# Features-first product pairs: three of five additions replaced by accumulation onto ScalarE copies in PSUM

## The chip, the core and the metric

The kernel runs on one core of a Trainium2 chip. The metric is the device time of a run in microseconds, lower is better; it is given as the median of several runs.

## The reference, cut to what matters

One layer of a gated decoder trunk on 1024 prompt rows and 8 sample rows (1032 in all), width 1024. One input projection with seven blocks of 1024 columns gives u, v, z_a, x_b, z_b, g_a and g_b. Branch A mixes a normalised v within chunks of 128 rows; branch B pools x_b over trailing windows. Two more projections merge them, then an output projection, a norm, and a gate with a per-layer embedding follow.

```python
proj = einsum('bld,de->ble', rmsnorm(h, pre_g), w_in)
u, v, z_a, x_b, z_b, g_a, g_b = split(proj, ...)
vn = layernorm(gelu(v), ln_g, ln_b)
y_a = gelu(u) * chunk_spatial_mix(vn, w_s, b_s) * silu(z_a)
y_b = pooled(x_b) * silu(z_b)
m = sigmoid(g_a) * (y_a @ w_pa) + sigmoid(g_b) * (y_b @ w_pb)
h = h + rmsnorm(m @ w_out, post_g)
h = h + rmsnorm(sigmoid(rmsnorm(h, ple_in_g) @ w_pg) * (p @ w_ple), ple_out_g)
```

## The kernel before, in words

**The pairs.** Every large projection is cut into pairs of 128 output features (four pairs for each of the nine: v, ga, u, za, xb, zb, gb, pa, pb). The result of a pair is two features by two halves of the rows, 512 and 520 (WIDE, which holds the 8 sample rows). `strassen` (L691) computes it with Winograd's scheme: seven products P1 to P7 instead of eight, each a sum of weights (A11, A12, A22, S1 to S4) by a sum of the activations (B11, B21, B22, T1 to T4). P1, P2 and P4 have 512 columns, the other four 520, issued as two pieces of 260 (`Features.pieces`). `product` (L663) issues 4 contraction blocks by 3 terms, since each operand is split into a high and a low part (`split`: a ScalarE copy and a VectorE subtraction).

**What happens to a product.** `evacuate` inside `strassen` (L701): P1 is copied by ScalarE from PSUM to a slot u (with eight zero columns from `none`); P6 is added onto u by VectorE; P7 plus u gives u7; P5 plus u7, P4 plus u7 and P3 plus u are results (`user.summed`); P2 accumulates in PSUM onto P1 and goes out by ScalarE with the pair's function (`user.direct`). That makes five VectorE additions. `finish` then applies the function (gelu, silu, sigmoid or none for xb) to the results that came by `summed`. For pa and pb (`Merge`, L1322, `MergeB`, L1339) `direct` is a VectorE multiplication by a reloaded gate.

**PSUM.** Three regions of two banks (`region`, tag "acc") and two single banks (`bank`); they are taken in turn.

**The operand sums.** x, turned to features by rows, lies in `big` (128 by 8 by 1032). `combine` (L525) overwrites quarters of it in place: T3 = B22 - B12 over B22, T1 = B12 - B11 over B12, T2 = B11 + T3 over B11, T4 = B21 - T2 over B21; `cut` splits each into slots. After that `big` serves as scratch: the eight chunks of v (`vtok`, L1005) and their spatial mix (`spatial`, L1118), which `ZA` (L1193) multiplies in; the pooling windows (`XB.window`, L1256) with four scratch rows; and at the end the merged result.

**What sets the order.** Every operation is recorded by a planner (`Planner`, `order`, L274) which then lays out all five queues: it estimates durations, gives each operation a due time, and takes on each engine, TensorE too, what can start soonest and is due first. `PUSH` moves due times of named operations. `run_stream` (L833) records the steps one product after another; weights are prepared AHEAD = 3 steps before use, loads fetched 6 steps before. The first three pairs of v are interleaved by `MERGED` with the order `EDGE`; the start up to product 6 is written out in `SCRIPT`, with embedding products (`embed`, L1697) and the operand sums between. 46 slots of SBUF hold everything that is not in `big`. All SBUF loads and stores are issued on SP's queue, two kinds of accumulating ones on POOL's. Because all operations are recorded, nearly every row of the profile has line 374.

**Branch B.** The steps of group g are the pair xb, the pair zb and `mixes(g)` (L1285), two further products; `mixes` is placed after the third product of the next group's xb pair, and yb is spilled three steps later (`store`, L1423).

Of the kernel before, what the change touches and what calls it, by code (L numbers as in the profile page):

```python
# [31 lines left out]
PUSH = {'hs': -4.0, 'norm': -5.0, 'half': 0.0, 'cut': -1.0, 'e': 2.0, 'we': -2.0, 'vw': -9.0, 'p': 3.0}  # L32
# [8 lines left out]
OS, GS = 5, 12  # L41
WINDOWS = (2, 4, 8, 16)
# [339 lines left out]
def hybrid_step(  # L382
# [12 lines left out]
    accp = ctx.enter_context(tc.tile_pool(name="accp", bufs=3, space=bass.MemoryType.PSUM))  # L395
    bankp = ctx.enter_context(tc.tile_pool(name="bankp", bufs=2, space=bass.MemoryType.PSUM))
    plan = Planner(nc, SLOTS, {"acc": 3, "bank": 2})
# [64 lines left out]
    big = cpool.tile([P, NB, T], F32, tag="big", name="big")  # L462

# [35 lines left out]
    class Operand:  # L499
# [5 lines left out]
                    "T1": (0, 1), "T2": (0, 0), "T3": (1, 1), "T4": (1, 0)}  # L505
# [9 lines left out]
        def cut(self, what):  # L515
            i, j = self.QUARTERS[what]
            for kk in range(2):
                hi, lo = self.new(what, kk)
                if what == "T2":
                    split(quarter(kk, 0), hi[:, :, :HALF], lo[:, :, :HALF])  # L520
                    split(quarter(2 + kk, 1)[:, :, HALF:], hi[:, :, HALF:], lo[:, :, HALF:])
# [94 lines left out]
    class Features:  # L616

        new = staticmethod(lambda: region("acc"))
# [3 lines left out]
        @staticmethod  # L622
        def view(ps, wide):
            return ps[:, :, :QT] if wide else ps[:, 0, :HALF]

        @staticmethod
        def pieces(ps, wide):
            if not wide:
                return [(ps[:, 0, :HALF], slice(0, HALF))]
# [5 lines left out]
    class Tokens:  # L635

        new = staticmethod(lambda: region("acct")[:, 0])
# [53 lines left out]
    def strassen(weights, operand, user, form=Features, order=None):  # L691
# [41 lines left out]
        for p, a, b, r in sorted(plan, key=lambda x: order.index(x[0])) if order else plan:  # L733
            def run(p=p, a=a, b=b, r=r):
                new = r not in at
                if new:
                    at[r] = form.new()
                product(form, at[r], weights.ready[a], operand, b, new, True, not new)

            steps.append(Step(lambda a=a: weights.prepare(a), run, lambda p=p: evacuate(p)))  # L740
        steps[0].loads = lambda: (weights.fetch(), user.loads())
# [3 lines left out]
    def strassen_within(weights, operand, user, order=None):  # L745
# [26 lines left out]
        for p, a, b, r in sorted(plan, key=lambda x: order.index(x[0])) if order else plan:  # L772
            def run(a=a, b=b, r=r):
                new = r not in at
                if new:
                    at[r] = Tokens.new()
# [188 lines left out]
    def x_half(j, kps):  # L965

        for kp in kps:
            two = region("pst") if kp != 1 else None
            ps = [bank("pst") if two is None else two[:, kk] for kk in range(2)]
# [35 lines left out]
    vtok = lambda t: sv if t == S else big[:, t, :D]  # L1005
# [856 lines left out]
```

## Time and profile before

| | |
|---|---|
| median of 3 runs | 978.66 us (976.48 to 979.82) |
| profiled execution | span 975.6 us from its first to its last instruction; the page gives no other time of it |
| TensorE (PE) busy | 963.1 us, 99% |
| weight loads (PEld) | 855.9 us, 88% |
| VectorE (DVE) busy | 813.4 us, 83% |
| ScalarE (ACT) busy | 497.9 us, 51% |
| GpSimd (POOL) busy | 74.2 us, 8% |
| granted TensorE clock, mean | 0.998 (the upper level, 2.4 GHz) |
| DMA | 185.82 MB |

Times are microseconds unless marked ns. Matmuls overlap in the records: the pace is read from start to start, not from the length of one. An engine's busy share says little by itself; what counts is what it waits for and who waits for it. A name such as `xT2h,uw` reads: high part of operand sum T2, weights of a u pair; `acc` is a PSUM accumulator of a pair, `acct` one of the output and gate stages, `pst` the turning of x, `e` the embedding.

### The profile page before, as it was taken

The page shows a single profiled execution, that of the slowest core. Times are in us where ns is not written, and L with a number is a line of the kernel's source. Part 1 is how long each engine was busy: PE and PEld are TensorE (multiplying, and loading weights), DVE is VectorE, ACT ScalarE, POOL GpSimd, SP SyncE. Part 2 cuts the span into 40 slices and gives each one's busy share as a digit, 9 for nine tenths or more (in the row PEclk, how much of TensorE's full clock was granted, in tenths as well). Part 3 has the DMA queues.
Part 4 walks back from the last instruction along what each step waited for, and adds up shares of the span by engine and source line. Part 5 has one row for each costly group of instructions (what it writes and reads, how often), then busy time and mean ns, then how long its engine had stood idle before and what let it go on. Part 6 is the DMA issues. An engine that isn't in the chain of part 4 may idle for free. (4 is left out here: it accounts for less than half of the span.)

```text
span 975.6 us, 15918 instructions
## 1 busy us (share of the span) xinstructions
PE 963.1 (99%) x6037; PEld 855.9 (88%) x6037; DVE 813.4 (83%) x1261; ACT 497.9 (51%) x852; POOL 74.2 (8%) x117
## 2 busy tenths in 40 slices
PE   8999999999999999999999999999999999999996
PEld 6789899999999999999999999999999997788775
DVE  6998568988889788868698897698699899779987
ACT  7664345766444443242434343563263274698655
POOL 2200000000000000000010100000000001323212
PEclk9999999999999999999999999999999999999999
DMA  9523955423467464453425366692492385799896
GB/s 327 172 105 68 192 124 183 155 97 119 164 226 261 136 203 160 140 195 120 152 99 183 134 214 238 228 384 89 158 382 92 111 301 189 151 299 313 224 320 215
DMA packets 128506, 185.82 MB, mean 190 GB/s; under 512 B 42150, under 2 KB 85198, under 8 KB 128421
## 3 DMA queue, kind: packets, MB, share of 16 engines
q1 hardware_dynamic: 126381, 177.43, 54.9%
q0 software_dynamic: 2048, 7.37, 4.1%
q8 instruction: 47, 0.77, 0.3%
q14 instruction: 30, 0.25, 0.1%
HBM read 129.27 MB, written 55.96 MB: 190 GB/s over the span
## 5 line engine op out<-in xcount | busy, mean ns | idle before, releaser
L374 DVE TENSOR_TENSOR u<-acc,u 128x520 f32<-128x520 f32 (+1 forms) x89 | 62.0, 696 | 35.5 <-PE acc L374 35.2
L374 POOL TENSOR_TENSOR rstd<-ms,mhalf 128x1 f32<-128x1 f32 (+1 forms) x37 | 30.9, 841 | 520.3 <-DVE ms L374 517.7
L374 ACT ACTIVATE u<-acc 128x512 f32<-128x512 f32 (+1 forms) x43 | 25.6, 596 | 44.2 <-PE acc L374 44.0
L374 DVE TENSOR_TENSOR big<-big 128x1024 f32<-128x1024 f32 (+4 forms) x20 | 23.8, 1219 | 0.0
L374 POOL COPY big<-xb 128x1 f32<-128x1 f32 x8 | 3.4, 419 | 260.4 <-ACT xb L374 219.7
L374 ACT ACTIVATE paw<-pas 128x512 fp32r<-128x512 f32 x16 | 10.0, 630 | 24.0 <-DVE pas L374 18.2
L374 ACT ACTIVATE pbw<-pbs 128x512 fp32r<-128x512 f32 x16 | 10.0, 628 | 22.1 <-DVE pbs L374 16.8
L374 PE MATMUL accm<-qh,wpoolw 128*128 128x260 f32 (+1 forms) x96 | 20.9, 319 | 0.0
L374 ACT ACTIVATE big<-mix 128x256 f32<-128x256 f32 x32 | 12.0, 382 | 17.1 <-PE mix L374 16.4
L374 ACT ACTIVATE gbw<-gbs 128x512 fp32r<-128x512 f32 x16 | 10.1, 630 | 19.3 <-DVE gbs L374 10.0
L374 DVE SCALAR_TENSOR_TENSOR zb<-accm,gvec,zb 128x512 f32<-128x512 f32 (+1 forms) x16 | 12.0, 754 | 9.4 <-PE accm L374 9.2
L374 ACT ACTIVATE zaw<-zas 128x512 fp32r<-128x512 f32 x16 | 10.0, 628 | 18.1 <-DVE zas L374 10.0
L374 ACT ACTIVATE junk<-h 128x512 bf16<-128x512 f32 x25 | 15.7, 628 | 3.4 <-DVE h L374 2.9
L374 PEld LDWEIGHTS accm<-qh,wpoolw 128*128 128x128 f32 x96 | 15.6, 188 | 1.9
L374 ACT ACTIVATE zbw<-zbs 128x512 fp32r<-128x512 f32 x16 | 10.1, 628 | 13.8 <-DVE zbs L374 8.2
L374 ACT ACTIVATE u<-acct 128x512 f32<-128x512 f32 x22 | 13.0, 589 | 7.4 <-PE acct L374 4.6
L374 DVE TENSOR_TENSOR paw<-pas,paw 128x512 fp32r<-128x512 f32 x16 | 10.9, 688 | 6.7 <-ACT paw L374 6.7
L374 ACT ACTIVATE mw<-ms 128x512 fp32r<-128x512 f32 x16 | 10.0, 625 | 12.4 <-DVE ms L374 9.7
L374 ACT ACT_TABLE_LOAD x11 | 14.1, 1283 | 4.0 <-PE acc L374 2.3
L374 ACT ACTIVATE zbw<-zbraw 128x512 fp32r<-128x512 f32 x12 | 7.5, 623 | 16.6 <-DMA zbraw<-in_w_in_dram 10.7
L374 ACT ACTIVATE gbw<-gbraw 128x512 fp32r<-128x512 f32 x12 | 7.4, 624 | 16.4 <-DMA gbraw<-in_w_in_dram 14.3
L374 PE MATMUL mix<-wst,vh 128*128 128x256 f32 x64 | 15.5, 320 | 0.0
(655 smaller groups left out, 3560.5 us busy)
## 6 DMA issues: line engine op xcount, KB each, us to landing
ga<-ga SPq DMA_DIRECT2D x16, 516.0 KB, 4.6
gb<-gb SPq DMA_DIRECT2D x16, 516.0 KB, 6.2
ya<-za SPq DMA_DIRECT2D x8, 516.0 KB, 3.6
yb<-zb SPq DMA_DIRECT2D x8, 516.0 KB, 4.5
x<-in_x_prompt_dram SPq DMA_DIRECT2D x8, 512.0 KB, 9.3
vraw<-in_w_in_dram SPq DMA_DIRECT2D x8, 512.0 KB, 6.4
e<-e SPq DMA_DIRECT2D x8, 512.0 KB, 3.6
vturned<-v SPq DMA_DIRECT2D x32, 128.0 KB, 4.5
```

Of the source, the lines that this page charges most:

```text
L374: getattr(getattr(self.nc, e), method)(*(self.real(a) for a in args), **{k: self.real(a) for k, a in kwargs.items()})
```

## The change

A new function `seeded` takes the place of `strassen` for all pairs but the first three of v, in the order P1, P7, P6, P2, P5, P4, P3. ScalarE copies P1 from its single bank into a double one (in two pieces and eight zero columns), and P6, P5 and P3 accumulate there one upon the other; P7 is copied to a slot w. VectorE adds w to the double bank after P6 and writes the sum into the second single bank, upon which P4 accumulates. So P2, P4 and P3 go out by `direct`, P5 alone by `summed`. PSUM becomes two fixed double banks (`acc`), two fixed single ones (`one`) and two of `bank`. The operand sums are written differently (T1 first, then T2 = B22 - T1 over the same place, T3 = T2 - B11, T4 = B21 - T2), and B22 is not overwritten. The spatial mix is stored to DRAM chunk by chunk and loaded back by rows of features; the chunks and the window scratch use fewer rows of `big`. `mixes` stands after the whole next xb pair (LATE = 7), with its accumulators in `bank` and `acc`, and the store of yb right behind it. Evacuations of the new pairs are due 2.0 us earlier for the planner. The rest adapts names; the diff is cut to its core.

```diff
+PUSH = {..., 'out': 2.0}
+LATE = 7
+PST = (0, None, 2, 1)
...
-    plan = Planner(nc, SLOTS, {"acc": 3, "bank": 2})
+    plan = Planner(nc, SLOTS, {"bank": 2})
...
+    def banks(i):
+        return one if i == 2 else [acc[i][:, q] for q in range(2)]
...
-    def region(name):
-
-        n_name[0] += 1
-        return plan.tile(accp.tile([P, 2, 512], F32, tag="acc", name=f"{name}_{n_name[0]}"), "acc")
+    acc = [plan.tile(accp.tile([P, 2, 512], F32, tag=f"acc{i}", name=f"acc{i}"), "acc") for i in range(2)]
+    one = [plan.tile(accp.tile([P, 512], F32, tag=f"one{i}", name=f"one{i}"), "acc") for i in range(2)]
...
+    flat = big.rearrange("p b t -> p (b t)")
+    KEPT = 8 * WIDE
...
-                    "T1": (0, 1), "T2": (0, 0), "T3": (1, 1), "T4": (1, 0)}
+                    "T1": (0, 1), "T2": (0, 1), "T3": (0, 0), "T4": (1, 0)}
...
-                if what == "T3":
-                    sub(b22, b22, b12)
-                elif what == "T1":
+                if what == "T1":
                     sub(b12[:, :, :HALF], b12[:, :, :HALF], b11)
                 elif what == "T2":
-                    add(b11, b22[:, :, :HALF], b11)
+                    sub(b12, b22, b12)
+                elif what == "T4":
+                    sub(b21, b21, b12[:, :, :HALF])
                 else:
-                    sub(b21, b21, b11)
+                    sub(b11, b12[:, :, :HALF], b11)
...
     class Features:
-        new = staticmethod(lambda: region("acc"))
+        new = staticmethod(lambda wide: turn("wide", acc) if wide else turn("one", one))
...
     class Tokens:
-        new = staticmethod(lambda: region("acct")[:, 0])
+        new = staticmethod(lambda wide: turn("tokens", [one[0], acc[0][:, 0], one[1], acc[1][:, 0]]))
...
+    def seeded(weights, operand, user):
+
+        steps, at, cut = [], {}, (slice(0, QT), slice(QT, HALF))
+        plan_of = (("P1", "A11", "B11"), ("P7", "S3", "T3"), ("P6", "S2", "T2"), ("P2", "A12", "B21"),
+                   ("P5", "S1", "T1"), ("P4", "A22", "T4"), ("P3", "S4", "B22"))
+
+        def evacuate(p):
+            one, four, two, seven = at["r1"], at["r4"], at["r2"], at["r3"]
+            if p == "P1":
+                for q, c in enumerate(cut):
+                    nc.scalar.activation(out=two[:, q, : c.stop - c.start], in_=one[:, c], func=AF.Copy)
+                nc.scalar.activation(out=two[:, 1, HALF - QT : QT], in_=none, func=AF.Copy)
+            elif p == "P7":
+                at["w"] = slot("w", (P, WIDE))
+                nc.scalar.activation(out=Features.like(at["w"]), in_=Features.view(seven, True), func=AF.Copy)
+            elif p == "P6":
+                for q, c in enumerate(cut):
+                    add(four[:, c], two[:, q, : c.stop - c.start], at["w"][:, c])
+            elif p == "P2":
+                user.direct(0, 0, one)
+            elif p == "P5":
+                w = Features.like(at["w"])
+                user.summed(1, 1, Features.view(two, True), w, w)
+            elif p == "P4":
+                user.direct(1, 0, four)
+            elif p == "P3":
+                user.direct(0, 1, Features.view(two, True))
+
+        for p, a, b in plan_of:
+            def run(p=p, a=a, b=b):
+                if p == "P1":
+                    first = turn("pair", (0, 1))
+                    at.update(r1=one[first], r4=one[1 - first], r2=acc[0], r3=acc[1])
+                r = {"P1": "r1", "P2": "r1", "P4": "r4", "P7": "r3"}.get(p, "r2")
+                new = p in ("P1", "P7")
+                product(Tokens if r in ("r1", "r4") else Features, at[r], weights.ready[a], operand, b,
+                        new, True, not new)
+
+            steps.append(Step(lambda a=a: weights.prepare(a), run, lambda p=p: pushed("out", evacuate, p)))
...
-    vtok = lambda t: sv if t == S else big[:, t, :D]
+    vtok = lambda t: sv if t == S else flat[:, KEPT + t % 4 * D : KEPT + (t % 4 + 1) * D]
...
+        dma(kept["mix"][:, t * P : (t + 1) * P].rearrange("(h p) t -> p h t", p=P),
+            vtok(t).rearrange("p (h t) -> p h t", h=NB))
...
-                zt, mixed = z[:, :SEQ].rearrange("p (t c) -> p t c", c=P), big[:, :, b * P : (b + 1) * P]
+                mixed = slot("mixed", (P, SEQ))
+                dma(mixed, kept["mix"][b * P : (b + 1) * P, :])
+                zt, mixed = (a.rearrange("p (t c) -> p t c", c=P) for a in (z[:, :SEQ], mixed))
...
-            s, free = x, [big[:, 2 * i, :], big[:, 2 * i + 1, :]]
+            s, free = x, [flat[:, KEPT + n * T : KEPT + (n + 1) * T] for n in range(2)]
...
-                    ps = held[m, j] = region("accm")
+                    plan.apart()
+                    ps = held[m, j] = acc[1 - m] if j else bank("accm")
...
-        vsteps.append(strassen(w, xop, u, order=EDGE if i < EDGES else None))
+        vsteps.append(strassen(w, xop, u, order=EDGE) if i < EDGES else seeded(w, xop, u))
...
-        steps += x[:3] + late + x[3:] + z
+        steps += x[:LATE] + late + x[LATE:] + z
...
-        at(follow[5], store)
+        at(bsteps[g][2][1], store)
...
-    PARTS = ("B11", "T2", "B21", "T3", "T4", "T1", "B22")
+    PARTS = ("B11", "T3", "T2", "B21", "T1", "T4", "B22")
...
-            for what in ("T3", "T1", "T2"):
+            xop.combine("T1")
+            xop.cut("T1")
+            xop.combine("T2")
+            xop.cut("T2")
+            for what in ("T3", "T4"):
                 xop.combine(what)
-            xop.cut("T2")
-            xop.combine("T4")
-            for what in ("T3", "T1", "T4"):
                 xop.cut(what)
```

## Rows read from the trace of the kernel before

**Rows 1.** The page's part 1: span, busy time, share and instructions of each engine.

```profile
span 975.6 us, 15918 instructions
PE 963.1 (99%) x6037; PEld 855.9 (88%) x6037; DVE 813.4 (83%) x1261; ACT 497.9 (51%) x852; POOL 74.2 (8%) x117
```

**Rows 2.** Waits of TensorE: waiter, releaser, us in total, times, longest us.

```profile
PE warm L374 <- DVE heat L374: 1.5, 1, 1.5
PE e L374 <- ACT wehi L374: 1.2, 1, 1.2
PE pst L374 <- DVE big L374: 0.7, 1, 0.7
PE acct L374 <- ACT ge L374: 0.6, 1, 0.6
PE acc L374 <- DVE big L374: 0.3, 1, 0.3
```

**Rows 3.** The chain that ended last: start us, us, what.

```profile
966.20 1.35 PE acct L374 x9
```

**Rows 4.** Timeline of TensorE, 300 to 345 us: first matmuls of four products.

```profile
301.77 0.40 PE L374 MATMUL acc<-xT2h,uw 128*128 128x260 f32 x2
...
304.65 0.39 PE L374 MATMUL acc<-xB21h,uw 128*128 128x512 f32 x1
...
315.95 0.39 PE L374 MATMUL acc<-xB11h,zaw 128*128 128x512 f32 x1
...
318.73 0.40 PE L374 MATMUL acc<-xB22h,uw 128*128 128x260 f32 x2
```

**Rows 5.** Timeline of TensorE, 105 to 126 us: first matmuls of three products.

```profile
115.20 0.40 PE L374 MATMUL acc<-xT4h,vw 128*128 128x512 f32 x1
...
117.97 0.40 PE L374 MATMUL acc<-xT1h,vw 128*128 128x260 f32 x2
...
120.82 0.40 PE L374 MATMUL acc<-xB11h,gaw 128*128 128x512 f32 x1
```

**Rows 6.** Stretches: length, busy of PE, PEld, DVE, ACT, POOL; clock, DMA share, GB/s.

```profile
105.00:125.00 20.00, 20.00 (x129) 18.00 (x129) 8.49 (x14) 6.64 (x14) 0.00 (x0) 1.00 0.90 189
300.00:340.00 40.00, 40.00 (x269) 36.89 (x269) 33.70 (x50) 19.20 (x29) 0.00 (x0) 1.00 0.62 209
```

**Rows 7.** Groups by shape, VectorE then ScalarE: busy us, mean ns, idle before.

```profile
L374 DVE TENSOR_TENSOR u<-acc,u 128x520 f32<-128x520 f32 x85 | 59.2, 697 | 34.8 <-PE acc L374 34.5
...
L374 DVE TENSOR_TENSOR big<-mix,big 128x256 f32<-128x256 f32 x32 | 12.9, 421 | 2.0 <-ACT big L374 1.5
...
L374 ACT ACTIVATE u<-acc 128x512 f32<-128x512 f32 x40 | 23.8, 595 | 38.8 <-PE acc L374 38.6
...
L374 ACT ACTIVATE big<-mix 128x256 f32<-128x256 f32 x32 | 12.0, 382 | 17.1 <-PE mix L374 16.4
...
L374 ACT ACTIVATE za<-za 128x1032 f32<-128x1032 f32 x4 | 4.3, 1064 | 4.2 <-DVE za L374 4.2
```

**Rows 8.** Waits of ScalarE for a product, before its work on u.

```profile
ACT u L374 <- PE acc L374: 51.0, 33, 4.0
```

**Rows 9.** Timeline of ScalarE: two weight splits that waited for a load.

```profile
484.52 0.63 ACT L374 ACTIVATE zbw<-zbraw 128x512 fp32r<-128x512 f32 x1 [7.66 <-DMA zbraw<-in_w_in_dram]
...
544.66 0.63 ACT L374 ACTIVATE gbw<-gbraw 128x512 fp32r<-128x512 f32 x1 [7.00 <-DMA gbraw<-in_w_in_dram]
```

**Rows 10.** Timelines of VectorE and TensorE in the start: operand sums, cuts, first T3.

```profile
42.49 1.24 DVE L374 TENSOR_TENSOR xB22l<-big,xB22h 128x1040 fp32r<-128x1040 f32 x1
...
45.53 4.66 DVE L374 TENSOR_TENSOR big<-big 128x1040 f32<-128x1040 f32 x4
50.11 2.38 DVE L374 TENSOR_TENSOR xT3l<-big,xT3h 128x1040 fp32r<-128x1040 f32 x2
...
57.96 0.41 PE L374 MATMUL acc<-xT3h,vw 128*128 128x260 f32 x2
```

**Rows 11.** DMA issues: KB each, median us from issue to landing.

```profile
vblocks<-vturned SPq DMA_DIRECT2D x8, 512.0 KB, 6.0
```

More of the change, by code (lines that the diff above doesn't have):

```diff
@@ L31 @@
 WE = 1
-PUSH = {'hs': -4.0, 'norm': -5.0, 'half': 0.0, 'cut': -1.0, 'e': 2.0, 'we': -2.0, 'vw': -9.0, 'p': 3.0}
+PUSH = {'hs': -4.0, 'norm': -5.0, 'half': 0.0, 'cut': -1.0, 'e': 2.0, 'we': -2.0, 'vw': -9.0, 'p': 3.0, 'out': 2.0}
 WARM = 9
@@ L518, in cut @@
                 hi, lo = self.new(what, kk)
-                if what == "T2":
+                if what == "T3":
                     split(quarter(kk, 0), hi[:, :, :HALF], lo[:, :, :HALF])
-                    split(quarter(2 + kk, 1)[:, :, HALF:], hi[:, :, HALF:], lo[:, :, HALF:])
+                    split(quarter(kk, 1)[:, :, HALF:], hi[:, :, HALF:], lo[:, :, HALF:])
                 else:
@@ L623, in view @@
         def view(ps, wide):
-            return ps[:, :, :QT] if wide else ps[:, 0, :HALF]
+            return ps[:, :, :QT] if wide else ps
         @staticmethod
@@ L736, in run @@
                 if new:
-                    at[r] = form.new()
+                    at[r] = form.new(r not in ("r1", "r5"))
                 product(form, at[r], weights.ready[a], operand, b, new, True, not new)
             steps.append(Step(lambda a=a: weights.prepare(a), run, lambda p=p: evacuate(p)))
+        steps[0].loads = lambda: (weights.fetch(), user.loads())
+        steps[-1].after.append(user.finish)
+        return steps
+    def seeded(weights, operand, user):
[33 more added lines that the diff above has]
+            steps.append(Step(lambda a=a: weights.prepare(a), run, lambda p=p: pushed("out", evacuate, p)))
@@ L775, in run @@
                 if new:
-                    at[r] = Tokens.new()
+                    at[r] = Tokens.new(False)
                 product(Tokens, at[r], weights.ready[a], operand, b, new, True, not new)
@@ L967, in x_half @@
         for kp in kps:
-            two = region("pst") if kp != 1 else None
-            ps = [bank("pst") if two is None else two[:, kk] for kk in range(2)]
+            ps = [bank("pst") for _ in range(2)] if kp == 1 else banks(PST[kp])
             for i in range(4):
@@ L1150, in hybrid_step @@
     kept["h"] = dram.tile([T, D], F32, tag="h", name="h")
+    kept["mix"] = dram.tile([D, SEQ], F32, tag="mix", name="mix")
     kept["e"] = dram.tile([T, D], F32, tag="e", name="e")
@@ L1220, in pool_state @@
     def pool_state():
[L1221 removed]
+        dma(state_sb[: NS * POOL_BUF], state.rearrange("b r d -> (b r) d"))
     def small_tables():
@@ L1387, in hybrid_step @@
     for g, (x, z, mix) in enumerate(bsteps):
-        steps += x[:3] + late + x[3:] + z
+        steps += x[:LATE] + late + x[LATE:] + z
         late = mix
-    steps += gbsteps[0][:3] + late + gbsteps[0][3:]
+    steps += gbsteps[0][:LATE] + late + gbsteps[0][LATE:]
     steps += [s for p in gbsteps[1:] + pasteps + pbsteps for s in p]
@@ L1420, in hybrid_step @@
             at(bsteps[g][1][1 + 2 * i], lambda u=u, i=i: u.window(i))
-        follow = bsteps[g + 1][0] if g + 1 < NPAIR else gbsteps[0]
         def store(g=g):
@@ L1699, in embed @@
         hi, lo = pcut[q // 2]
-        ps = e_ps[q, n] = region("e")
+        e_ps[q, n] = turn("e", (0, 1, 2))
+        ps = banks(e_ps[q, n])
         for i in range(2):
@@ L1708, in embed @@
                     plan.apart()
-                nc.tensor.matmul(ps[:, i], p, w, start=j == 0, stop=j == 5)
+                nc.tensor.matmul(ps[i], p, w, start=j == 0, stop=j == 5)
     def embed_out(q, n, fast=False):
@@ L1713, in embed_out @@
         ps = e_ps.pop((q, n))
-        if fast:
-            nc.vector.tensor_copy(e, ps)
-        else:
-            nc.scalar.activation(out=e, in_=ps, func=AF.Copy)
+        for o, i in [(e, acc[ps])] if ps < 2 else [(e[:, i], one[i]) for i in range(2)]:
+            if fast:
+                nc.vector.tensor_copy(o, i)
+            else:
+                nc.scalar.activation(out=o, in_=i, func=AF.Copy)
         rows = kept["e"][q // 2 * HALF : (q // 2 + 1) * HALF].rearrange("(p t) c -> p t c", t=4)
```

27 lines of the change are left out of this document (15 added, 12 removed).

## The prediction, made before the changed kernel was run

> **What bounds the kernel now.** I read the busy shares first. TensorE is busy 963.1 of 975.6 us, VectorE 813.4, ScalarE 497.9 [rows 1]. A 99% share could still hide stalls, so the waits of TensorE come next: they add up to 4.3 us, of which 1.5 us is the first instruction's and 2.8 us all that follows [rows 2]. The chain of waits gives the tail: the last nine matmuls end at 966.20 + 1.35 = 967.55, and 8 us of ScalarE and VectorE work on the last output tile follow, which the diff does not touch [rows 3]. So of 12.5 us without TensorE, about 9.5 are head and tail, and some 3 us are left between.
>
> Then the pace. In a stretch in the middle a wide product (24 matmuls of 260 columns) takes 304.65 - 301.77 = 2.88 us, a narrow one (12 of 512) 318.73 - 315.95 = 2.78 [rows 4]. The same rows show the planner's order: P1 of the next pair (B11, za) runs before P3 of this one (B22, u). A product that waits for an evacuation is moved behind one that doesn't.
>
> Is that pace TensorE's own, or does VectorE's traffic slow it? In 105 to 125 us VectorE is busy 8.49 of 20 us (42%), in 300 to 340 us 33.70 of 40 (84%) [rows 6]. In the first stretch a narrow product takes 117.97 - 115.20 = 2.77 us and a wide one 120.82 - 117.97 = 2.85 [rows 5]. The pace doesn't follow VectorE's load. Only less TensorE work or fewer waits can shorten this kernel.
>
> The Trainium skill (VectorE: DVE Perf Modes, section on the TRN2 errata) gives a matmul as max(60, 6 + columns) cycles at 2.4 GHz, which makes 216 ns of 512 columns. The trace disagrees: 2.78 / 12 = 232 ns, so measured numbers stand. By the page some 7% of the products' time would be something other than TensorE, and an engine that is relieved could give it back; that is the third rival.
>
> **The change part by part.** *TensorE's work.* Each pair keeps seven products with the same columns: P1, P2, P4 as one piece of 512, the others as two of 260. The mixes keep theirs. Cost 0.
>
> *VectorE.* 33 pairs take the new form (one of v; four each of ga, u, za, xb, zb, gb, pa, pb). A pair had five additions of about 0.697 us [rows 7], 3.49 us. Now it has P5's, 0.70, and the sum into P4's bank in two halves; the nearest row is the 256-column addition from PSUM, 0.421 us, so 0.84. That saves 3.49 - 1.54 = 1.95 us a pair, 64 us in all: 813 falls to about 749 us (77%). Everything saved is beside TensorE, which after its first instruction waits for VectorE twice, 1.0 us, both before 41 us while x is turned [rows 2]. Worth on the path: 0.
>
> *ScalarE.* A pair adds the copy of P1 in two pieces (2 x 0.382 in place of 0.595), the copy of P7 (0.60), and P4 and P3 straight from PSUM (2 x 0.60), while the finish shrinks from 1032 + 520 columns to 520 (minus 1.06) [rows 7]: +0.9 us. For xb there is no finish to save (+1.97), and for pa and pb P4 and P3 stay on VectorE (+0.77). 21 x 0.9 + 4 x 1.97 + 8 x 0.77 = 33 us; 498 rises to 531 us (54%). It lies beside TensorE. The price of a ScalarE copy into PSUM has no row: below by 0, above by the 512-column copy, 0.6 us; I take 0.382, the same length read from PSUM.
>
> *New waits.* Two accumulators are now filled by another engine before TensorE goes on, and four single and double regions are fixed. In the written order each has one product of cover:
> - P6 adds onto the copy of P1; cover P7, 2.88 us. The copy needs 2 x 0.38 and a short instruction for eight zero columns, under 0.38: 1.15. Slack 1.7.
> - P5 overwrites what the halved addition reads, and P4 adds onto what it writes; cover P2, 2.78, need 0.84. Slack 1.9.
> - P3 adds onto what P5's addition reads; cover P4, 2.78, need 0.70. Slack 2.1.
> - P1 of the next pair takes the bank that P4 left; cover P3, 2.88, need 0.60. Slack 2.3.
> - P6 of the next pair also needs P3's evacuation ahead of the P1 copy; cover two products, 5.66, need 1.6.
>
> These slacks hold if the engines come promptly. Today they do: 33 times ScalarE sat idle for a product's end before its work on u [rows 8], 38.6 us of it before the copy of P1, and VectorE 34.5 us before its additions from PSUM [rows 7]. VectorE, with 8% less to do, will be prompter, ScalarE a little less. Queued behind ScalarE's new evacuations are the weight splits, which the code prepares three products ahead (AHEAD). Estimate: 0 to 2 us of new waits in all.
>
> *The start.* T3, which is used first, was a single subtraction; it becomes the last of three (T1, T2, T3), with T1's cut between, since T2 overwrites T1's place. Today VectorE subtracts four times from 45.53 to 50.19, cuts T3 to 52.49, and TensorE starts on T3 at 57.96: cover 5.5 us [rows 10]. The new chain is three sums of two (4.66 / 4 = 1.17 each) and two cuts of two (2.38 each): 7.0 + 4.8 = 11.8 us. B22's cut no longer stands ahead of it, because nothing overwrites B22 now, so it can begin about where that cut stood, near 42.5, and end near 54.3, still 3.7 us early. Bounds: 0, and 2.4 us less cover if B22's cut stays ahead; even then 1.3 us is left. I take 0.
>
> *The mix through DRAM.* Eight stores and eight loads of 512 KB on SP's queue. The nearest row is the 512 KB block reload, 6.0 us to land [rows 11]. A store waits for the last addition of its chunk, with weight loads behind it on SP; VectorE waits for a load if it is late. The cover is the weights' lead, and ZA's result is only needed pairs later. 0, above one late landing of 6 us.
>
> *Scratch, LATE, store, Tokens.* The two windows of a pair now share two buffers, so the second waits for the first one's split; POOL's small copies and SP's spills go past it unhurried. The mixes move four products later, the spill and reload of yb stand right behind them; q and zb hold slots about 11 us longer, and "w" frees its slot sooner than "u" did. Four token banks in place of three may remove the 0.6 us before acct [rows 2]. PSUM in the start keeps as many accumulators as are open at a time. Together -0.6 to +2 us; I take 0.
>
> **The sum.** Work 0, waits -0.5 to +2, taken as +0.5: span 976.1. The page gives the span, and no time of its own beside it; the runs' median stands 978.66 - 975.6 = 3.1 us above. 976.1 + 3.1 = **979.2 us**, no measurable change. A measurement of this kernel tells about 0.3% (2.9 us) from no change.
>
> **Rivals.** *ScalarE is held by a late load (slower).* A queue runs in order. Today ScalarE stands 7.66 us before a weight split until zbraw lands, and 7.00 us for gbraw [rows 9]; it costs nothing, because it had only P1 and P2 to evacuate. Now nearly every product needs it. The mechanism decides where the hold lasts more than 1.7 us past the end of P1. These two would cost up to 7.66 - 1.7 and 7.00 - 1.7, 11.3 us. Against it: the planner may put the evacuations ahead (it is told to, by 2.0), and part of the idle time had nothing else to run. At about half, +6 us: 985. Chance 0.24.
>
> *The start runs dry (slower).* T1's two cuts wait for ScalarE's halves, and VectorE's work there follows without a gap [rows 10]. If B22's cut stays ahead (1.3 us of cover left) and the six operations of S2's and S3's weights fall ahead of T3 too, each near an addition [rows 7] (6 x 0.69 = 4.1), TensorE waits 2.8 us: 979.2 + 2.8 = 982.0. Chance 0.08.
>
> *TensorE is relieved (faster).* If VectorE's traffic slowed the products, 64 us less of it would show. The two stretches bound it [rows 4, 5]: 2.77 against 2.78 and 2.85 against 2.88 for 42 points of load, at most 1% (10 us), of which 7 points are worth under 2 us. With it the 2.8 us of waits [rows 2] gone: 974. Chance 0.05.
>
> *Only the waits go (faster).* All 2.8 us [rows 2] and no new one: 978.7 - 2.8 = 975.9, at the edge of what can be told. Chance 0.12.
>
> The forecast keeps 0.51. **Chances:** faster by over 0.3% (below 975.7): 0.05, half of the 0.12, and 0.05 of the forecast's own spread, 0.16. Slower (above 981.6): nearly all of 0.24 + 0.08, 0.31. Within 0.3%: the rest, 0.53. **Range:** from 975.5, just under what the waits alone give, to 987, the held ScalarE at half and a little beyond.
>
> **What would show it.** Right: VectorE near 750 us, ScalarE near 530, TensorE still near 963, its waits under 6 us, products of 2.78 and 2.88. A wrong step shows as waits of TensorE for "acc" or "one" on ScalarE (first rival), for T3 or T2 on VectorE around 58 us (second), or as products shorter than 2.75 us (third). The forecast falls if TensorE's idle time between 60 and 960 us grows by more than 3 us.

## The result, and the profile after

The changed kernel takes 982.87 us (median of 16 runs, 980.92 to 984.45) where the kernel before took 978.92 in the same comparison (976.48 to 981.51): a ratio of 1.0042, 95% interval 1.0033 to 1.005. It is **slower by 0.4%, 4 us**. The forecast was 979.2, no measurable change; the result lies in its range (975.5 to 987) and outside its middle: the side above 981.6 had a chance of 0.31.

The page after, its part 1 (busy time, share of the span, instructions; before: [rows 1]):

```profile
span 981.1 us, 16020 instructions
PE 965.5 (98%) x6037; PEld 858.0 (87%) x6037; DVE 759.5 (77%) x1195; ACT 528.0 (54%) x949; POOL 67.2 (7%) x117
```

VectorE has lost 54 us of busy time, ScalarE has gained 30, TensorE issues the same 6037 matmuls, and the span is 5.5 us longer. Not all of that is the change's: in the runs on record an execution's time stands 1.7 us above its span (982.83 and 981.1 here), so the execution of the kernel before that was profiled is one of about 977.3 us, 1.6 under its median. The medians differ by 4.0 us, and the spans of these two executions by 1.5 us more. The six longest waits of TensorE after (waiter, releaser, us in total, times, longest; before: [rows 2]):

```profile
PE one L376 <- ACT u L376: 1.8, 1, 1.8
PE warm L376 <- DVE heat L376: 1.5, 1, 1.5
PE one L376 <- DVE hw L376: 0.8, 1, 0.8
PE acc L376 <- ACT u L376: 0.7, 1, 0.7
PE acc L376 <- DVE big L376: 0.6, 1, 0.6
PE one L376 <- ACT ge L376: 0.6, 1, 0.6
```

Three are new, 1.8, 0.8 and 0.7 us. The timeline puts them at 879.82, 910.69 and 938.24 us: none is in the pairs that were rewritten, all are in the output and gate stages, whose arithmetic the diff leaves alone. First the part that was rewritten, in the timeline of TensorE after (start, us, engine, line, operation): the first T3 product, the starts of three products of one pair in the middle, and the first product of the output stage.

```profile
56.63 0.40 PE L376 MATMUL acc<-xT3h,vw 128*128 128x260 f32 x2
...
298.43 0.40 PE L376 MATMUL one<-xB11h,uw 128*128 128x512 f32 x1
...
301.23 0.41 PE L376 MATMUL acc<-xT3h,uw 128*128 128x260 f32 x2
...
304.12 0.40 PE L376 MATMUL acc<-xT2h,uw 128*128 128x260 f32 x2
...
800.10 0.39 PE L376 MATMUL one<-woB11h,mw 128*128 128x512 f32 x1
```

A narrow product takes 301.23 - 298.43 = 2.80 us, a wide one 304.12 - 301.23 = 2.89, within 0.02 of [rows 4]. The pairs end at 800.10. The kernel before, in the same view, runs the output stage's P1 ahead of its last pair product:

```profile
797.43 0.39 PE L374 MATMUL acct<-woB11h,mw 128*128 128x512 f32 x1
...
800.20 0.41 PE L374 MATMUL acc<-ybB22h,pbw 128*128 128x260 f32 x2
...
803.08 0.40 PE L374 MATMUL acct<-woT3h,mw 128*128 128x512 f32 x1
```

Less that P1 (800.20 - 797.43 = 2.77), its pairs end at 803.08 - 2.77 = 800.31. **Over the first 800 us, in which everything but the turn of banks was changed, the kernels are 0.2 us apart.** From there to the end of the span the kernel before takes 975.6 - 800.3 = 175.3 us, the changed one 981.1 - 800.1 = 181.0. All of the loss is made after the rewritten part. By stages (output stage, gate stage, tail behind the last product) the 175.3 us are 83.3, 84.0 and 8.0, and the 181.0 are 86.95, 85.0 and 9.0: most of it is lost in the output stage.

What happens there is in the chain of waits after (start, us, what):

```profile
852.73 7.52 DMA h<-in_x_prompt_dram
...
867.40 7.58 DMA hblocks<-h
...
875.05 1.26 DVE big L376
...
877.30 1.05 ACT wgT2h L376
...
879.19 0.58 ACT u L376
...
879.82 4.61 PE one L376 x12
```

POOL's accumulating load of x into a finished tile h takes 7.5 us. The spill of h follows; then ScalarE and VectorE reduce the tiles to their norms and SP issues other transfers, some 7 us in all; then comes the load of the blocks, and VectorE stands in its queue until they land, to turn them.

The chain names only the last releaser of each step, and the transfer of x was not the only one. In the timeline and the waits of SP's queue after (852 to 862 us), a weight load between the two spills of h stood 5.6 us until TensorE released it, and only the last 2.0 us before the second spill went to x:

```profile
851.29 0.34 SPq L376 DMA_DIRECT2D h<-h  x1
851.73 6.44 SPq L376 DMA_DIRECT2D wgB<-wg  x2
860.27 0.34 SPq L376 DMA_DIRECT2D h<-h  x1
...
SPq L376 <- PE one L376: 5.6, 1, 5.6
SPq L376 <- DMA h<-in_x_prompt_dram: 2.0, 1, 2.0
```

Before, both spills go out ahead of the weight loads, the second one 5.5 us earlier (851.96 + 3.18 = 855.14 against 860.61):

```profile
851.96 3.18 SPq L374 DMA_DIRECT2D h<-h  x2
855.24 0.39 SPq L374 DMA_DIRECT2D wgB<-wg  x1
```

So two things hold the spill up, the order of SP's queue and the transfer of x, which POOL issues at 852.73 us where the kernel before issues it at 849.52.

At the other end of the chain ScalarE has a weight split next in its queue, which the profile lets go with VectorE's turn at 875 us (it probably takes a buffer that the turn frees; the trace doesn't say):

```profile
876.33 2.01 ACT L376 ACTIVATE wgT2h<-wgT 128x1024 fp32r<-128x1024 f32 x2 [2.88 <-DVE big L376]
```

Behind that split stands the copy of P5 (u), whose product ended at 875.06. So P3 finds its bank taken. In the timeline of VectorE after, the two turns of hblocks that stood longest (idle before, and what ended it, in brackets):

```profile
866.98 1.25 DVE L376 STREAM_TRANSPOSE big<-hblocks 128x1024 f32<-128x1024 f32 x1 [1.10 <-DMA hblocks<-h]
...
875.05 1.25 DVE L376 STREAM_TRANSPOSE big<-hblocks 128x1024 f32<-128x1024 f32 x1 [2.95 <-DMA hblocks<-h]
```

and the one of before in that stretch:

```profile
867.92 1.25 DVE L374 STREAM_TRANSPOSE big<-hblocks 128x1024 f32<-128x1024 f32 x1 [0.71 <-DMA hblocks<-h]
```

Why do 3 us of VectorE matter, when it is busy 77% of the run? The same stretch of both kernels (length, busy of PE, PEld, DVE, ACT, POOL; clock, DMA share, GB/s), before and after:

```profile
862.00:912.00 50.00, 49.92 (x220) 39.95 (x219) 47.52 (x70) 41.61 (x74) 14.25 (x11) 1.00 0.93 279
```

```profile
862.00:912.00 50.00, 47.42 (x202) 37.57 (x201) 42.45 (x64) 39.50 (x73) 9.96 (x13) 0.97 0.84 258
```

Before, VectorE worked 47.52 of these 50 us beside a TensorE that was busy for 49.92: two full engines side by side. Even before the change the chain of waits, which the view follows back no further than 895.93 us, runs along VectorE for its first 14 us:

```profile
896.58 2.23 DVE wgT4l L374 x2
...
907.40 1.50 DVE hw L374 x3
...
911.71 14.13 PE acct L374 x60
```

In the changed kernel VectorE's idle time there is 7.55 us in place of 2.48, 5.1 more, about what the span has grown by.

TensorE's own order is no cause of it: from 806 us to the sample rows' products of the gate stage (925.77 us before, 929.87 after) both kernels issue the same products in the same order, but for eight small ones of the sample rows that change places with one product, and there the changed kernel is already 4.1 us behind. What differs up to there is the banks the products write and the order on the other queues, as on SP's above.

### The profile page after: what moved, and what is told of

It is laid out like the page before. It is cut to its first block, busy times and chain, and to the rows that moved or that the text cites. A ratio compares the mean times of both kernels' runs of the same rounds, so it can differ in the third digit from the quotient of the medians.

```text
span 981.1 us, 16020 instructions
## 1 busy us (share of the span) xinstructions
PE 965.5 (98%) x6037; PEld 858.0 (87%) x6037; DVE 759.5 (77%) x1195; ACT 528.0 (54%) x949; POOL 67.2 (7%) x117
## 4 chain that ended last, share of the span: by engine, by line
PE 85%; DVE 6%; DMA 4%; ACT 1%; issue 1%; SPq 1%; POOL 0%; DVEq 0%; ACTq 0%
PE acc L376 46%; PE one L376 36%; DMA hblocks<-h 3%; DVE big L376 2%; PE mix L376 1%; PE accm L376 1%; SPq L376 1%; DMA vecs<-in_ple_in_g_dram 1%; DMA h<-in_x_prompt_dram 1%; ACT junk L376 1%; DVE vw L376 1%; DVE vs L376 1%; PE sps L376 0%; DVE ge L376 0%; DVE xB22l L376 0%
## 5 line engine op out<-in xcount | busy, mean ns | idle before, releaser
L376 DVE TENSOR_TENSOR one<-acc,w 128x260 f32<-128x260 f32 x66 | 28.5, 432 | 24.5 <-PE acc L376 23.3
L376 ACT ACTIVATE acc<-one 128x260 f32<-128x260 f32 x66 | 24.3, 369 | 38.2 <-PE one L376 37.0
L376 ACT ACTIVATE w<-acc 128x520 f32<-128x520 f32 x33 | 19.9, 603 | 32.5 <-PE acc L376 32.5
L376 ACT ACTIVATE acc<-none 128x8 f32<-128x8 f32 x33 | 5.9, 179 | 27.2 <-DVE zb L376 10.6
L376 ACT ACTIVATE u<-acc 128x512 f32<-128x512 f32 (+1 forms) x17 | 10.2, 601 | 17.3 <-PE acc L376 12.8
L376 ACT ACTIVATE junk<-h 128x512 bf16<-128x512 f32 x25 | 15.7, 627 | 4.9 <-DVE h L376 2.6
L376 ACT ACTIVATE xbw<-xbs 128x512 fp32r<-128x512 f32 x16 | 10.1, 630 | 14.6 <-DVE xbs L376 13.2
L376 ACT ACTIVATE u<-one 128x512 f32<-128x512 f32 x23 | 13.6, 592 | 7.9 <-PE one L376 6.2
L376 DVE TENSOR_TENSOR gbw<-gbs,gbw 128x512 fp32r<-128x512 f32 x16 | 10.9, 689 | 8.6 <-ACT gbw L376 8.3
L376 ACT ACTIVATE uw<-us 128x512 fp32r<-128x512 f32 x16 | 10.0, 628 | 12.6 <-DVE us L376 7.0
```

The lines of the kernel that those rows point to most:

```text
L376: getattr(getattr(self.nc, e), method)(*(self.real(a) for a in args), **{k: self.real(a) for k, a in kwargs.items()})
```

## The experiments

The theory: the rewritten pairs cost nothing, and the loss is made after 800 us by the order in which the planner lays the last two stages out. The pairs leave it another state, and the output and gate stages now take four banks in turn where they took three. The rivals: the four banks cost the time themselves; the new pairs cost it in some way that shows late. Each kernel was timed in five rounds against the kernel before.

### The old pairs on the new PSUM

```diff
-    vsteps.append(strassen(w, xop, u, order=EDGE) if i < EDGES else seeded(w, xop, u))
+    vsteps.append(strassen(w, xop, u, order=EDGE if i < EDGES else None))
...
-    gasteps = [seeded(
+    gasteps = [strassen(
```

(and so for u, za, xb, zb, gb, pa and pb)

> The changed kernel with the five-addition pairs of before (P1, P6, P2, P7, P4, P5, P3) in the new PSUM frame; all else stays. If the new pairs cost the 4 us (ScalarE's evacuations late), the stretch from the first ga product to the end of the last pb product gets shorter by 3 us or more and the time falls to about 979. If the loss lies behind the pairs, as I now think, that stretch stays within 1 us of 680 us, VectorE rises by some 60 us to about 820, and the time is set by whatever the last 180 us do: between 978 and 984.

Measured: 988.07 us, ratio 1.0092 (1.0074 to 1.011): worse than the whole change, by 5 us, and above what either side expected. Busy time of VectorE is back at 814.0 us. The pairs end at 800.45 by the same reckoning, so the old form and the new one cost TensorE the same; the loss is again behind them, at another place. In the timeline of TensorE:

```profile
933.22 1.88 PE L376 MATMUL sps<-wgrow,sst 128*8 128x512 f32 x4 [4.11 <-DMA wgrow<-wg]
```

Here TensorE itself waited 4.1 us for a load. What follows: in the pairs the old additions cost no more than the new ones; whatever costs sits in PSUM's new layout, the turn of banks, or the order.

### Three banks in the turn

```diff
-    turn("tokens", [one[0], acc[0][:, 0], one[1], acc[1][:, 0]])
+    turn("tokens", [one[0], acc[0][:, 0], one[1]])
```

> The changed kernel with three token banks in turn in place of four in the output and gate stages. If the fixed turn of four banks costs the last stage its time, the stretch from the first output product to the last matmul falls from 172 to about 167.5 us, total near 979. If the loss is a late block load that VectorE and ScalarE stand behind, the number of banks is no cause: the wait of P3 for ScalarE stays, or moves elsewhere, total 981 to 985.

Measured: 980.84 us, ratio 1.0023 (1.0012 to 1.0035), half of the loss regained by the medians, just between the two expectations; the interval touches that of the changed kernel (1.0033 to 1.005). VectorE's idle time in 862 to 912 us is 4.67. Its longest stand for hblocks, 3.51 us at 869.84, is longer than the 2.95 us of the changed kernel, and yet TensorE's longest wait in the output stage is 0.78 us: the length of such a stand does not by itself decide what it costs.

### One due time moved, in both kernels

```diff
-TURNS = ((7, 8, 11), (14, 14, 18), (21, 26, 28), (30, 33, 35))
+TURNS = ((7, 8, 11), (14, 14, 20), (21, 26, 28), (30, 33, 35))
```

The due time is that of the turn of hblocks that stood 2.95 us. In the changed kernel:

> The changed kernel with the turning of h blocks 3 and 2 asked for two products later (third number of the second entry of TURNS 20 in place of 18). If VectorE's stand of 2.95 us for the block load near 875 us is what holds ScalarE's copy, TensorE's 1.8 us wait there goes, and with it the stretch of half clock behind it (1.65 us): 979.4, 3.5 us less. If the wait has another cause, it stays and the time is 982 to 984.

Measured: 983.99 us, ratio 1.0054 (1.004 to 1.0067). The stand at 875 us is gone, TensorE's wait of 1.8 us with it, and the output stage, from 800.65, ends at 884.13: 83.5 us against 86.95 in the changed kernel. It came back in the gate stage (86.8 us in place of 85.0) and in the tail behind the last product (11.5 in place of 9.0). In the kernel before:

> Control: the kernel before with the same two-product delay. It has no such stand (0.71 us there), so nothing to win: within 1 us of 978.9 if the delay acts only through that stand; about 975.5 if the delay is good by itself.

Measured: 982.84 us, ratio 1.0051 (1.0032 to 1.0071). The control was to stand still and lost the same 4 us as the whole change, from one number of the planner; its own runs spread from 980.25 to 989.37. In the timeline of ScalarE:

```profile
942.12 0.64 ACT L374 ACTIVATE hw<-big 128x512 fp32r<-128x512 f32 x1 [5.82 <-DMA out_dram<-ge]
```

So the kernel before is no sturdier in its last stages; its order is merely a good one.

### A slower DMA in the plan

If the stands come from loads that land later than planned, planning with slower loads should take them away.

```diff
-                pipe = max(pipe, end) + o.moved / (self.RATE if end > 26 else 0.41)
+                pipe = max(pipe, end) + o.moved / (0.27 if end > 790 else self.RATE if end > 26 else 0.41)
```

> The changed kernel; the planner alone, which lays the order out, reckons the bytes of every load after 790 us of its plan at 0.27 instead of its usual rate, so that work that needs a late block stands further back in the order. No computation and no buffer changes. Theory (the loss is work laid out behind block loads that land later than planned): VectorE's and ScalarE's long stands for loads after 850 us go, from the end of the last pair product to the span's end 175 to 177 us (181.0 in the changed kernel), time 977 to 980. Rival A (the four banks in turn are the cause themselves): 981 to 984 as in the changed kernel. Rival B (any new order of the last 180 us scatters by some us, with no rule): anywhere from 979 to 988.

Measured: 1008.8 us, ratio 1.0314 (1.0299 to 1.0328). With three banks as well:

> As the run before, and only three banks in the turn of the output and gate stages. Theory of late loads: the same 977 to 980, since three or four banks matter only through the order. Rival A (the four banks): 979 to 981, 2 us under the run with four banks and the same rate. Rival B (scatter): anywhere from 978 to 988.

Measured: 999.97 us, ratio 1.0222 (1.0207 to 1.0236). And on the kernel before:

> The kernel before the change with the same slower rate in the plan after 790 us. Theory of late loads: its last stretch has few stands for loads, so it keeps 976.5 to 979. Rival B (any new order costs): 980 to 985, as the kernel before with one due time moved did.

Measured: 1006.04 us, ratio 1.0287 (1.0272 to 1.0302). All three missed, far outside every theory's numbers: the remedy is wrong. Waits of TensorE in the first of them (as above):

```profile
PE one L376 <- ACT hw L376: 10.0, 1, 10.0
PE acc L376 <- ACT hw L376: 4.5, 1, 4.5
```

Its pairs end at 800.99; the loss is once more behind them. With a slower DMA in the plan, loads are also issued later (four loads of wgB at 881.80 us, 873.20 in the changed kernel), and the engines then truly wait for them. What stands is that the order alone, with the same instructions on every engine, is worth up to 28 us in the last 180 (1006.0 against 977.7 for the kernel before in that comparison), what TensorE loses by a lower clock after its waits included.

### The weight loads behind the block loads

```diff
-    turn_over(wgop, [*outsteps[2][4:], *l], [*l[2:], c[0], c[1]], WITHIN)
+    turn_over(wgop, [outsteps[2][6], outsteps[2][6], outsteps[2][6], *l], [*l[2:], c[0], c[1]], WITHIN)
```

> The changed kernel; the loads of the gate's second weight block on SP's queue may go no earlier than the seventh product of the last output group, so that the accumulating load of x behind them isn't held up by them. Theory of late loads: the accumulating load is issued near 849 us instead of 852.7, the block loads behind it land some 4 us earlier, VectorE's stand of 2.95 us at 875 us goes, the output stage ends near 883.5 instead of 887.0; 978 to 980 unless the weights now land too late. Rival A (four banks) and rival B (scatter): 981 to 986, the stand comes back at another place.

Measured: 982.27 us, ratio 1.0043 (1.0029 to 1.0056). The output stage ends at 883.81, as expected; the accumulating load was issued no earlier (853.16 us; it is on POOL's queue, not behind the weight loads), but the spill behind it on SP's queue was, by 1.5 us, the blocks landed sooner, and VectorE stood 1.63 us for them in place of 2.95. SP now stands 6.8 us for x at that spill. All of that was lost in the tail: the last product ends at 968.74, and 12.8 us follow in place of 9.0, in which VectorE is still at the sample rows and the last tiles. Together with three banks:

> The changed kernel with both edits that each regained a part: three banks in the turn, and the loads of the gate's second weight block no earlier than the seventh product of the last output group. Theory, if the gains are of different waits: output stage 83.3 us as with the later loads, gate stage 84.5 and tail 8.0 as with three banks, span 976.3, time 979 to 980.5, as the kernel before. Any new order may cost again: up to 985.

Measured: 981.06 us, ratio 1.0021 (1.001 to 1.0033): no better than three banks alone. The gains don't add up.

### The late transfer taken away, the order kept

```diff
-            for e, (method, args, kwargs) in self.order():
+            for e, (method, args, kwargs) in [c for c in self.order() if c[1][2].get("accum_op") is None or c[1][2]["out"].tensor.name[:2] != "h_"]:
```

The only experiment that leaves the order of every engine as it is, and takes away a transfer that VectorE stood for. (In the expectation below, "882 to 884" for rival A is a slip: the changed kernel's time is 982 to 984.)

> The changed kernel with the order of every engine kept, and eight instructions left out: POOL's accumulating loads of x into the eight prompt tiles h of the output stage (so x isn't added to h). Nothing else differs, PSUM and the four banks in turn included. Theory (the loss is VectorE and ScalarE standing behind block loads, which wait for the spill of h, which waits for that accumulating load): the spill is issued some 7 us earlier, VectorE's stand of 2.95 us for hblocks at 875 us and TensorE's wait of 1.8 us behind it go, P2 and P3 of the last output group take 2.8 us again in place of 4.76 and 4.45, the output stage ends near 883.5 instead of 887.0, and the run at 977.5 to 980. Rival A (PSUM or the four banks cost the time themselves): 882 to 884, as the changed kernel.

Measured: 981.81 us, ratio 1.0028 (1.0017 to 1.0039). The control:

> The kernel before the change with the same eight loads left out and its order kept: the control. Theory: its output stage has hardly a stand for hblocks (0.71 us at 868 us), so it gains at most its few waits, 975.5 to 978.5; the difference to the changed kernel with the same left out falls from 4 us to 2 or less. Rival A: the difference stays 4 us.

Measured: 977.1 us, ratio 0.998 (0.9971 to 0.9989). VectorE's stands in the changed kernel without the loads:

```profile
867.59 1.25 DVE L376 STREAM_TRANSPOSE big<-hblocks 128x1024 f32<-128x1024 f32 x1 [1.86 <-DMA hblocks<-h]
...
873.86 1.25 DVE L376 STREAM_TRANSPOSE big<-hblocks 128x1024 f32<-128x1024 f32 x1 [1.23 <-DMA hblocks<-h]
```

Half a hit. The stand that made TensorE wait fell to 1.23 us, the wait at 880 fell to 0.39, and the output stage took 884.30 - 800.38 = 83.9 us in place of 86.95. But the other stand grew, the two together fell only from 4.05 to 3.09 us, and in the next stretch TensorE met a VectorE that was late:

```profile
909.27 0.73 PE L376 MATMUL one<-wgT2h,hw 128*128 128x512 f32 x2 [1.77 <-DVE hw L376]
```

The span fell by 1.3 us (981.1 to 979.8), not by 3 to 5, and the difference to the control stayed at 4.7 us, which is what rival A had said. Taking that one transfer away took that one wait away, and not the loss.

It didn't take the late spill away either: that was to go some 7 us earlier and went 1.7 us earlier. In the timeline and the waits of SP's queue in this kernel:

```profile
858.58 0.42 SPq L376 DMA_DIRECT2D h<-h  x1
...
SPq L376 <- PE one L376: 11.7, 1, 11.7
```

The weight load ahead of the spill now stands for TensorE until 858.1 us (857.8 in the changed kernel). So this run and the one with the later weight loads each remove one of two holds of nearly the same length, and what the changed kernel takes without both is not shown.

The same stretch in this kernel and in the control:

```profile
862.00:912.00 50.00, 47.79 (x209) 37.70 (x209) 43.77 (x65) 40.55 (x74) 6.37 (x9) 1.00 0.72 238
```

```profile
862.00:912.00 50.00, 50.00 (x222) 40.15 (x221) 48.13 (x72) 41.59 (x74) 10.67 (x7) 1.00 0.74 249
```

VectorE's idle time there is 6.23 us (7.55 with the loads): 1.3 less, as the span.

### Only the pairs' priorities changed

```diff
-    'out': 2.0}
+    'out': 0.0}
```

> The changed kernel with one number of the planner changed: the evacuations of the new pairs are put ahead by 0 instead of by 2 us (PUSH 'out'). The output and gate stages don't use the number, their order can only change through the state in which the planner reaches them. Theory (the pairs are free, the last stages are sensitive to any new order): the end of the last pair product within 1 us of 800.1; what follows anywhere from 175 to 186 us, total 977 to 988. Rival C (the early evacuations of the pairs are what holds TensorE's cost at nothing): the pairs get longer by over 1 us.

Measured: 987.7 us, ratio 1.0093 (1.0078 to 1.0109). The pairs end at 802.02, 1.9 us later: so putting the evacuations ahead is worth that much. Here the theory missed (within 1 us) and rival C hit (over 1 us): the pairs are free only with their evacuations put ahead. The other 2.6 us of its span's 4.5 over the changed kernel come after 800 us, where the edited number isn't used; TensorE waits 3.5 us there for a load of wgrow.

### All of them in one table

From the stretches of VectorE in each profile: its work from 862 us to the end of the span, its idle time in 862 to 912 us (50 less its busy time) and from 912 us to the end. For kernels that run the output stage's P1 ahead, 2.77 us are taken off the end of the pairs. All columns but the median are of one execution each, which lies up to 1.8 us off its median.

| kernel | median us | pairs end | VectorE's work from 862 | idle 862 to 912 | idle from 912 | span |
|---|---|---|---|---|---|---|
| before, loads of x left out | 977.1 | 799.7 | 99.2 | 1.9 | 11.7 | 974.8 |
| before | 978.9 | 800.3 | 99.2 | 2.5 | 11.9 | 975.6 |
| three banks | 980.8 | 800.5 | 98.2 | 4.7 | 12.5 | 977.4 |
| three banks, weights late | 981.1 | 800.3 | 98.9 | 4.9 | 13.1 | 978.9 |
| changed, loads of x left out | 981.8 | 800.4 | 98.0 | 6.2 | 13.6 | 979.8 |
| weights late | 982.3 | 800.5 | 98.6 | 5.7 | 15.2 | 981.5 |
| before, due time 20 | 982.8 | 799.9 | 99.2 | 6.3 | 13.2 | 980.7 |
| **changed** | 982.9 | 800.1 | 98.1 | 7.6 | 13.4 | 981.1 |
| changed, due time 20 | 984.0 | 800.7 | 98.5 | 6.3 | 15.7 | 982.4 |
| pushed by 0 | 987.7 | 802.0 | 99.3 | 6.3 | 18.0 | 985.6 |
| old pairs | 988.1 | 800.5 | 99.0 | 5.7 | 20.1 | 986.8 |
| three banks, rate 0.27 | 1000.0 | 801.0 | 99.4 | 8.1 | 29.1 | 998.6 |
| before, rate 0.27 | 1006.0 | 800.3 | 100.0 | 6.4 | 35.1 | 1003.5 |
| rate 0.27 | 1008.8 | 801.0 | 101.2 | 8.0 | 35.9 | 1007.1 |

VectorE has 98 to 101 us of work left at 862 us in every kernel, and its last instruction ends 3.5 us before the span does (972.1 of 975.6 before, 977.6 of 981.1 after); the rest is the last stores. So the span is 862 us, that work, and its idle time; that is arithmetic and says no more than that the work hardly differs and the idle time does. Down to the changed kernel, the one with late weights aside, the first idle column differs more than the second: what VectorE loses in 862 to 912 us is not made up for later. The dearer ones lose after 912 us, to loads that TensorE or ScalarE waits for. An idle VectorE is partly a consequence, since it also waits for a TensorE that stands; the table shows where the time goes and not alone who began. Who began is shown for the wait at 880 us alone, by the chain and by the runs that shorten the stand.

No version beat the kernel before: the fastest changed one that computes everything, with three banks, stands at 1.0023. That the loss lies in the last two stages is shown. That it is the planner's order is made likely by the controls, which lose as much from one number, and is not shown apart from PSUM's fixed banks: no run has the new banks and the old order. How the loss divides between the four banks (2 us, when taken back alone, which is less than the control moved), the fixed banks and the state that the new pairs leave the planner stays open. A run with the new pairs and the last two stages held to the order of before would settle it; it wasn't tried.

## Why the prediction was right and wrong

**TensorE bounds the kernel: right for 800 of 980 us.** 33 pairs have the old pace, and the run with the old pairs ends them within 0.4 us of the same point.

**VectorE and ScalarE beside it: the sizes right, the cover not everywhere.** The durations of VectorE's groups add up to 64 us less, as worked out; its busy time falls by 54, because instructions back to back overlap in the profile, as these two of the start do (52.21 + 0.68 is past 52.81):

```profile
52.21 0.68 DVE L376 TENSOR_TENSOR vs<-vs,vraw 128x512 f32<-128x512 f32 x1
52.81 2.35 DVE L376 TENSOR_TENSOR xT3l<-big,xT3h 128x1024 fp32r<-128x1024 f32 x2
```

ScalarE went to 528 us (531 forecast). The new operations in the page's costliest groups (count, busy us, mean ns, idle before; pieces of 260 and of 252 columns are one group):

```profile
L376 DVE TENSOR_TENSOR one<-acc,w 128x260 f32<-128x260 f32 x66 | 28.5, 432 | 24.5 <-PE acc L376 23.3
L376 ACT ACTIVATE acc<-one 128x260 f32<-128x260 f32 x66 | 24.3, 369 | 38.2 <-PE one L376 37.0
L376 ACT ACTIVATE w<-acc 128x520 f32<-128x520 f32 x33 | 19.9, 603 | 32.5 <-PE acc L376 32.5
```

The copy into PSUM, which had no row, was taken at 0.382 and is 0.369. The Trainium skill (ScalarE: Activation LUTs, "Step-by-step: what each stage is for") says that ScalarE writes PSUM faster than SBUF; the trace agrees in sign, by 13 ns: the copies of 256 columns from PSUM into SBUF took 382 [rows 7], these, of 256 columns in the mean, 369.

**The new waits: right.** Between 80 and 878 us TensorE is busy for 798.00 of 798 us, so the cover of one product per handover (1.7 to 2.3 us of slack) held 33 times. The run with no push shows that it was not free of the planner: without the evacuations put ahead the pairs take 1.9 us more.

**The start: right.** T3's cut ends at 52.81 + 2.35 = 55.16 (54.3 forecast), and TensorE comes to T3 at 56.63, earlier than [rows 10]: 1.5 us of cover were left, not 3.7. **The mix through DRAM: right**, no wait of TensorE lies there. The 0.6 us before acct, which four banks were to remove, are still there as "one" on "ge".

**The step that failed** is "Scratch, LATE, store, Tokens. ... Together -0.6 to +2 us; I take 0". Of these four only Tokens, the turn of four banks, acts in the last two stages, and the planner's new order there has no term at all. The two stages and the tail came out 181.0 - 175.3 = 5.7 us longer, with the clock's share of 1.65 (last section). That is the span's miss, 981.1 where the sum had 976.1: 5.7, less the 0.5 of new waits that the sum had put into the pairs and that didn't come, less the 0.2 by which the pairs end sooner. By the medians the miss is 3.7 us (982.9 against 979.2). Behind it stands a reading: that VectorE and ScalarE lie beside TensorE was argued from shares of the whole run and from two stretches, both in the pairs [rows 6]. No stretch of the last 180 us was read. One question for the stretch 862 to 912 us would have shown 47.52 of 50, and the chain of before running along VectorE. By the forecast's own test, TensorE's idle time between 60 and 960 us growing by over 3 us, it falls: TensorE is busy for 896.47 of these 900 us in place of 899.92, and P3 ran 1.65 us longer besides.

**That the result lies in the range is luck.** The range's upper part was there for ScalarE held by a late load in the pairs, and that didn't happen; the 4 us came from stages for which the sum had no cost.

**The rivals.** "ScalarE is held by a late load", 985 us with 0.24, named the kind of mechanism (a queue that stands, with evacuations behind it) at the wrong place and on the wrong engine: VectorE stood for the load, and ScalarE behind VectorE, in the gate's weight splits. Where it was priced the hold did not come: ScalarE's longest stand for a load in the pairs is 2.63 us (zbraw at 475.99); in the kernel before it was 7.66 us [rows 9]. Its time was 2 us too long. "TensorE is relieved" is out: with 54 us less of VectorE the products are no shorter, 2.80 / 12 = 233 ns. "The start runs dry" and "only the waits go" did not happen.

The Trainium skill (Perfetto Trace Analysis, "Identifying the Most-Contended Engine") advises to find the engine with the highest occupancy, for TensorE not by its matmuls but, among others, by the busy share of its weight loads, and to work on that one first. Over the whole run that is TensorE before (88% against VectorE's 83%) and after (87% against 77%); in the stretch 862 to 912 us before the change it is VectorE, with 47.52 us against 39.95 us of weight loads.

## What to carry to other kernels

Work that was saved beside a full engine was worth nothing here, and a kernel with several stages has several bounds: ask of each stage, and not of the run, which engines are full, before you write "beside TensorE" next to a cost. A change that hands an automatic planner another state or other buffers has also changed every stage behind it; where two engines are full at once, its order there can be worth as much as the change itself or more (0.4 to 3% here, at equal work). So time an edit of such a kernel with a control that only shakes the order: an effect of that control's size says nothing on the edit.

## What the runs showed of the hardware

After TensorE's wait of 1.82 us at 879.82 us, its granted clock fell. The stretches from 880 us on (columns as above):

```profile
880.00:882.00 2.00, 2.00 (x5) 1.55 (x6) 1.97 (x4) 1.53 (x2) 0.87 (x1) 0.50 1.05 409
882.00:884.00 2.00, 2.00 (x7) 1.58 (x6) 2.00 (x3) 2.00 (x7) 0.00 (x0) 0.66 1.05 393
884.00:890.00 6.00, 6.00 (x27) 4.87 (x26) 6.00 (x8) 5.50 (x9) 0.00 (x0) 1.00 1.06 316
```

0.50 is the lower of its two levels, 1.2 of 2.4 GHz. P3 took 884.27 - 879.82 = 4.45 us in place of 2.80, so a wait of 1.82 us cost 1.65 more (timeline of TensorE):

```profile
879.82 0.70 PE L376 MATMUL one<-woB22h,mw 128*128 128x512 f32 x1 [1.82 <-ACT u L376]
...
884.27 0.39 PE L376 MATMUL acc<-woT4h,mw 128*128 128x512 f32 x1
```

The wait of 1.77 us at 909.27 us in the run without the loads of x cost nothing of the kind; the clock stayed at 1.00. The length of the wait alone doesn't decide it: the clock also stayed at 1.00 after waits of 1.96 us (three banks, weights late, at 894.86) and of 3.46 us (pushed by 0, at 933.60), and it fell to 0.50 after one of 2.48 us (before, due time 20, at 894.08). What tells them apart no run here shows.
